# The branch for overfull experts stands at the end of its layer, and TensorE gets products that nobody reads

## The chip, the cores and the metric

One core of a Trainium2 chip runs the whole kernel. The metric is the time of one execution on the device, in microseconds, as the median of several runs. The time before is 2018.78 us, the median of three runs (2011.02, 2018.78 and 2019.69). The profiled execution is a run of its own: 2027.7 us, with a span of 2025.7 us from its first instruction to its last.

## The reference, cut to what matters

256 tokens of width 1024 pass through two networks, one after the other, in float32. The first has two layers. Each is an attention (the first a dilated one over three patterns, the second a "stick-breaking" one), a norm, a mixture of 16 experts with two chosen for each token, and a norm again:

```
x = layer_norm(ALPHA * x + attention(x))
x = layer_norm(ALPHA * x + sum over the two chosen experts e of
               weight[e] * (silu(x @ gate[e]) * (x @ up[e])) @ down[e])
```

The second network has two layers, each with a gated feed-forward part, a mixing part (a recurrence over the tokens, retention, latent attention and a short convolution side by side) and a second feed-forward part.

How many tokens an expert gets depends on the data. Nothing in the reference limits it.

## The kernel before, in words

**Products.** Most matrices are split into a high and a low part of a reduced float32 format (`split`, lines 238 to 241: ScalarE writes the high part, VectorE the difference), and a product is three products on TensorE (`mm3`, lines 243 to 247). A single product is `mm`, lines 249 and 250. Weights come by SyncE's queue into a ring of four raw tiles (`fetch`, line 221), are split into rings of five `whi` and five `wlo` tiles, and are used. Because the rings are short, a weight's load waits until the tile's last reader is done.

**Order.** The program is written as one stream, and a framework orders it: for each engine it picks, instruction by instruction, what is ready by its own model of time, with the earlier line first, and sets the semaphores. `keep_in_program_order` and `issue_after` tie an instruction to its place, `manual_schedule` does so for all of VectorE's in a block. A tile that reuses the memory of another waits for the other's last reader. PSUM tiles come from three rings: `psA` (four banks in most stages), `psB` and `psC` (two each). Rows of 1024 come from two rings of four: `x` for the state between stages, taken in pairs, one for each half of the tokens (`new_x`), and `row` for everything else.

**The expert layer** (`moe`, from line 814). The weights of all experts, 96 loads of 512 KB, go through one ring of 22 homes: the raw tiles, the `whi` and `wlo` tiles (named `wf` here) and eight tiles of the layer's own. The router's scores come from `product` in `attention_out` (line 465). VectorE then ranks the experts (lines 859 to 878), TensorE counts each token's rank within its expert (line 891 reads it), and VectorE builds `P`, a matrix with a one where a token sits in one of 64 places of an expert. `gather` multiplies the split tokens (`xsh`, `xsl`) with `P` and so collects each expert's tokens: 32 products of 512 columns for the first eight experts, four for each block of 128 features; the first eight products (`t0`) stand ahead of the branch, the other 24 behind it. Then eight rounds, two experts in each: `up` (line 941), the gating (`hidden`), the second matrix, and `back`, which puts the results back on their tokens with `P` transposed; `add` (line 960) adds them to the state `x`, scaled by ALPHA the first time. The last two rounds are added at line 999, and `layer_norm` (from line 411) makes the next state `y`; its statistics (line 418) are written into the head of `y`. The norm of the second half of the tokens is left to the next stage (`rest`).

**The branch** (lines 921 to 923). An expert with more than 64 tokens does not fit into its places. The largest count is read into a register of each engine, and if it is over 64, `overflow` (line 1018) computes what was left out for all 16 experts, with weights that SyncE loads again into `row` tiles. With these inputs nobody takes the branch. Where it is skipped, each engine jumps over its part of the body and then raises its semaphores by what the body would have raised them. What comes later in the program and uses a tile that the body uses waits for these.

**Other stages that the change touches.** `dilated` (line 568) is the kernel's first stage. `stick` (line 678) is the second attention: ten steps, in which projections, scores (`weights`) and values of different head pairs overlap. `mixers` (line 1105) computes its column blocks with `chunk`; after the third and the fourth, `p8` collects the squared length of the keys by small products with `hsel`.

Of the kernel before, what the change touches and what calls it, by code (L numbers as in the profile page):

```python
# [169 lines left out]
class Net:  # L170
# [80 lines left out]

    def proj_b(self, out, w, c0, n, x, ks=range(8)):

        for k in ks:
            s = slice(c0 + k * n, c0 + (k + 1) * n)
            self.mm3(out, (w[0][:, s], w[1][:, s]), (x[0][:, k, :], x[1][:, k, :]), k == 0, k == 7)
# [181 lines left out]
    def attention_out(self, x, yT, w, l):  # L438
# [24 lines left out]
        def product(c):  # L463
            for k in range(8):
                self.mm(p[:, :16], xf[c][:, k * 128:(k + 1) * 128], self.gr[:, k, :], k == 0, k == 7)
# [102 lines left out]
    def dilated(self, c1):  # L568
        nc, A = self.nc, self.A
        with self.tc.tile_pool(name="dil", bufs=1) as sp, self.tc.tile_pool(name="dr", bufs=1, space=bass.MemoryType.DRAM) as dr:  # L570
            self.sp = sp
            nc.scalar.preload_act_table_set("exp_and_others")
            xT = self.new_T()
            xf = [self.row() for _ in range(2)]
# [103 lines left out]
    def stick(self, x):  # L678
        nc, A = self.nc, self.A
        with self.tc.tile_pool(name="sb", bufs=1) as sp:  # L680
# [79 lines left out]
            with self.psum(512) as self.pa:  # L760
                qk, z = {}, {}
                for hp in range(10):
# [6 lines left out]
                    if 1 <= hp <= 8:  # L769
                        z[hp - 1] = weights(*qk.pop(hp - 1))  # L770
                    if hp >= 2:
# [42 lines left out]
    def moe(self, x, l):  # L814
# [4 lines left out]
        with self.tc.tile_pool(name="moe", bufs=1) as sp, self.psum(512) as self.pa:  # L819
# [21 lines left out]

# [12 lines left out]
            h0, h1 = self.halves  # L854

# [64 lines left out]

            rv = nc.values_load(ci[0:1, 0:1], min_val=0, max_val=256)
            with self.tc.If(rv > 64):
                self.overflow(x, l, rank, gt)

# [35 lines left out]
            def add(ns):  # L960
                for c in range(2):
                    acc = [self.psA() for _ in range(2)]
                    back(acc, c, ns, True, True)
                    for s, a in zip(self.halves, acc):
                        stt(out=x[c][:, s], in0=x[c][:, s], scalar=1.0 if ns[0] else ALPHA, in1=a, op0=OP.mult, op1=OP.add)

            p = up(0)
            for n in range(8):
# [26 lines left out]
            y, gb = self.new_x(), self.ln_rows(l, 1)  # L995
            for c in range(2):
                with self.tc.issue_after(self.end.ins) if c else ExitStack():
                    for s, a in zip(self.halves, acc[c]):
                        tt(out=x[c][:, s], in0=x[c][:, s], in1=a, op=OP.add)
                if c == 0:  # L1000
                    self.layer_norm(x[0], gb, y[0], True)
        self.rest = lambda: self.layer_norm(x[1], gb, y[1])
# [15 lines left out]
    def overflow(self, x, l, rank, gt):  # L1018
# [4 lines left out]
        XT = sp.tile([128, 8, 1024], F32, name="XTo", tag="XT")[:, :, :256]  # L1023
        for c in range(2):
            for k in range(0, 8, 4):
# [3 lines left out]
                self.evac(XT[:, k:k + 4, c * 128:c * 128 + 128], t.rearrange("p (j s) -> p j s", j=4))  # L1029
        y = self.acc()  # L1030

        def load(ap):
            for j in range(2):
                raw = self.row()
                nc.sync.dma_start(out=raw, in_=ap[:, j * 1024:j * 1024 + 1024])
                yield raw

        for e in range(16):
            p = [self.psC() for _ in range(2)]
            for b in range(2):  # L1040
                for j, w in enumerate(load(self.A["egu"][l, e, b])):
# [702 lines left out]
```

## Time and profile before

| | before |
|---|---|
| median of three runs | 2018.78 us |
| profiled execution, time | 2027.7 us |
| its span | 2025.7 us |
| mean granted clock of TensorE | 0.968 |
| TensorE busy | 1919.8 us, 95% |
| VectorE busy | 1186.3 us, 59% |
| ScalarE busy | 862.8 us, 43% |
| read from HBM | 353.53 MB, 175 GB/s |

The page of the profile lists busy time by engine, then the span in 40 slices, then queues, a chain of waits and the costliest groups. PE is TensorE's products, PEld its loads of the stationary operand, DVE VectorE, ACT ScalarE, POOL GpSimd, SP SyncE; a q behind the name is that engine's sequencer. In a row, `out<-in` names the tiles; in square brackets stands the idle time of the engine ahead of the instruction and what ended it. PEclk is the share of 2.4 GHz that TensorE was granted.

### The profile page before, as it was taken

The page shows a single profiled execution, that of the slowest core. Times are in us where ns is not written, and L with a number is a line of the kernel's source. Part 1 is how long each engine was busy: PE and PEld are TensorE (multiplying, and loading weights), DVE is VectorE, ACT ScalarE, POOL GpSimd, SP SyncE. Part 2 cuts the span into 40 slices and gives each one's busy share as a digit, 9 for nine tenths or more (in the row PEclk, how much of TensorE's full clock was granted, in tenths as well). Part 3 has the DMA queues.
Part 4 walks back from the last instruction along what each step waited for, and adds up shares of the span by engine and source line. Part 5 has one row for each costly group of instructions (what it writes and reads, how often), then busy time and mean ns, then how long its engine had stood idle before and what let it go on. Part 6 is the DMA issues. An engine that isn't in the chain of part 4 may idle for free. (4 is left out here: it accounts for less than half of the span.)

```text
span 2025.7 us, 36997 instructions
## 1 busy us (share of the span) xinstructions
PE 1919.8 (95%) x14866; PEld 1622.0 (80%) x14866; DVE 1186.3 (59%) x2329; ACT 862.8 (43%) x1786; POOL 193.3 (10%) x225
## 2 busy tenths in 40 slices
PE   7999997997897997999999999999999999999998
PEld 7999996434885443899888988998999888888997
DVE  6778775125876124855576556555555675556554
ACT  5656552112662112544543335445544533235443
POOL 1323220000220000000021100000000030100000
PEclk9999998998998998999998999999999999899999
DMA  8345346795436796655532215555555532215553
GB/s 280 126 137 164 127 135 240 278 408 191 146 125 222 268 388 232 211 188 187 184 113 77 93 62 178 185 188 168 199 187 188 188 103 83 84 61 176 189 186 107
DMA packets 102516, 357.10 MB, mean 176 GB/s; under 512 B 11888, under 2 KB 15136, under 8 KB 102208
## 3 DMA queue, kind: packets, MB, share of 16 engines
q1 hardware_dynamic: 97584, 341.70, 49.1%
q10 hardware_dynamic: 4704, 12.81, 2.0%
q8 instruction: 120, 1.97, 0.4%
q14 instruction: 60, 0.49, 0.1%
q0 software_dynamic: 48, 0.13, 0.0%
HBM read 353.53 MB, written 1.07 MB: 175 GB/s over the span
## 5 line engine op out<-in xcount | busy, mean ns | idle before, releaser
L241 DVE TENSOR_TENSOR wlo<-raw,whi 128x512 fp32r<-128x512 f32 (+1 forms) x910 | 626.1, 715 | 384.0 <-ACT whi L240 380.1
L240 ACT ACTIVATE whi<-raw 128x512 fp32r<-128x512 f32 (+1 forms) x910 | 529.8, 616 | 592.3 <-issue 197.6
L245 PE MATMUL psB<-xTh,whi 128*128 128x256 f32 x1792 | 507.7, 283 | 12.3 <-ACT whi L240 8.3
L247 PE MATMUL psB<-xTh,wlo 128*128 128x256 f32 x1792 | 506.4, 283 | 0.2 <-DVE wlo L241 0.2
L246 PE MATMUL psB<-xTl,whi 128*128 128x256 f32 x1792 | 506.1, 282 | 0.4
L245 PEld LDWEIGHTS psB<-xTh,whi 128*128 128x128 f32 x1792 | 340.1, 190 | 18.1 <-ACT whi L240 9.8
L246 PEld LDWEIGHTS psB<-xTl,whi 128*128 128x128 f32 x1792 | 340.1, 190 | 5.4 <-DVE xTl L241 1.5
L247 PEld LDWEIGHTS psB<-xTh,wlo 128*128 128x128 f32 x1792 | 340.3, 190 | 1.4 <-DVE wlo L241 0.7
L247 PE MATMUL psA<-whi,hl 128*128 128x512 f32 x352 | 139.5, 396 | 0.0
L245 PE MATMUL psA<-whi,hh 128*128 128x512 f32 x352 | 139.4, 398 | 0.0
L246 PE MATMUL psA<-wlo,hh 128*128 128x512 f32 x352 | 138.7, 394 | 0.0
L245 PE MATMUL psA<-xTh,whi 128*128 128x256 f32 (+1 forms) x352 | 107.8, 307 | 0.3 <-ACT vt L536 0.2
L247 PE MATMUL psA<-xTh,wlo 128*128 128x256 f32 (+1 forms) x352 | 105.1, 299 | 0.0
L246 PE MATMUL psA<-xTl,whi 128*128 128x256 f32 (+1 forms) x352 | 103.6, 295 | 0.3 <-DVE xTl L241 0.3
L245 PE MATMUL psB<-whi,xTh 128*128 128x384 f32 (+2 forms) x256 | 90.3, 353 | 3.6 <-DVE qs L547 1.7
L247 PE MATMUL psB<-whi,xTl 128*128 128x384 f32 (+2 forms) x256 | 88.7, 347 | 0.4 <-DVE xTl L241 0.3
L246 PE MATMUL psB<-wlo,xTh 128*128 128x384 f32 (+2 forms) x256 | 88.5, 346 | 0.3 <-DVE wlo L241 0.3
L296 POOL TENSOR_TENSOR ss<-ss,mh 128x1 f32<-128x1 f32 x14 | 9.8, 702 | 785.5 <-DVE ss L295 780.8
L250 PE MATMUL psB<-raw,XT 128*64 128x512 f32 x288 | 83.5, 601 | 0.0
L247 PEld LDWEIGHTS psA<-whi,hl 128*128 128x128 f32 x352 | 66.0, 188 | 16.8 <-DVE hl L241 0.7
L246 PEld LDWEIGHTS psA<-wlo,hh 128*128 128x128 f32 x352 | 66.6, 189 | 12.6
L245 PEld LDWEIGHTS psA<-whi,hh 128*128 128x128 f32 x352 | 66.3, 188 | 12.8 <-ACT hh L240 0.9
(414 smaller groups left out, 3036.1 us busy)
## 6 DMA issues: line engine op xcount, KB each, us to landing
raw<-in_ffn1gu_dram SPq DMA_DIRECT2D x88, 512.0 KB, 3.8
raw<-in_ffn2gu_dram SPq DMA_DIRECT2D x88, 512.0 KB, 3.7
raw<-in_egu_dram SPq DMA_DIRECT2D x72, 512.0 KB, 9.9
wf<-in_egu_dram SPq DMA_DIRECT2D x56, 512.0 KB, 8.6
raw<-in_dqk_dram SPq DMA_DIRECT2D x46, 512.0 KB, 3.9
raw<-in_ffn1dn_dram SPq DMA_DIRECT2D x44, 512.0 KB, 3.6
raw<-in_ffn2dn_dram SPq DMA_DIRECT2D x44, 512.0 KB, 3.6
raw<-in_wb_dram SPq DMA_DIRECT2D x40, 512.0 KB, 3.7
```

The costliest lines, as they stand in the source:

```text
L240: self.hi = self.nc.scalar.activation(hi, src, AF.Copy)
L241: return (self.nc.gpsimd if pool else self.nc.vector).tensor_tensor(out=lo, in0=src, in1=hi.bitcast(F32), op=OP.subtract)
L245: mm(out, a[0], b[0], start=start, stop=False)
L246: mm(out, a[0], b[1], start=False, stop=False)
L247: mm(out, a[1], b[0], start=False, stop=stop)
L250: return self.nc.tensor.matmul(out, a, b, start=start, stop=stop)
L296: nc.gpsimd.tensor_tensor(out=ss[:, 3:4], in0=ss[:, 2:3], in1=self.mh[:, :1], op=OP.pow)
```

## The change

The branch moves from behind the first gathers to behind the last `back`. Its register is read after the first `up`. The layer's sum now grows in a pair of `x` tiles of its own, `z`, so that `x` stays as the branch needs it. The body of the branch handles the halves of the tokens one after the other, loads each expert's weights once for each half, takes the raw tiles for them in place of `row` tiles, and adds into `z`. A function `busy` issues products into a `psC` tile that nobody reads; it is called in `dilated` (four in float32 at the kernel's start), in `stick` (eight, once), in each expert layer (nine, tied behind the router's last product) and in each `mixers` (eight, behind its fourth column block).

```diff
--- before.py
+++ after.py
@@ -249,6 +249,13 @@
     def mm(self, out, a, b, start=True, stop=True):
         return self.nc.tensor.matmul(out, a, b, start=start, stop=stop)
 
+    def busy(self, n, a, b, behind=None):
+
+        with self.tc.issue_after(behind.ins) if behind is not None else ExitStack():
+            t = self.psC()
+            for _ in range(n):
+                self.mm(t[:, :b.shape[-1]], a, b)
+
     def proj_b(self, out, w, c0, n, x, ks=range(8)):
 
         for k in ks:
@@ -462,7 +469,7 @@
 
         def product(c):
             for k in range(8):
-                self.mm(p[:, :16], xf[c][:, k * 128:(k + 1) * 128], self.gr[:, k, :], k == 0, k == 7)
+                self.scored = self.mm(p[:, :16], xf[c][:, k * 128:(k + 1) * 128], self.gr[:, k, :], k == 0, k == 7)
             nc.vector.scalar_tensor_tensor(out=lg[:, c, :], in0=p[:, :16], scalar=mv[c][:, 2:3], in1=self.br, op0=OP.mult, op1=OP.add)
 
         acc = self.out_proj(yT, w, rows)
@@ -571,6 +578,9 @@
             self.sp = sp
             nc.scalar.preload_act_table_set("exp_and_others")
             xT = self.new_T()
+            w = self.row()[:, :512]
+            nc.gpsimd.memset(w, 1.0)
+            self.busy(4, w[:, :128], w)
             xf = [self.row() for _ in range(2)]
             for i in range(4):
                 nc.scalar.dma_start(out=xf[i // 2].rearrange("p (k t) -> p k t", k=4)[:, i % 2 * 2:i % 2 * 2 + 2, :],
@@ -768,6 +778,8 @@
                         self.tc.keep_in_program_order(nc.scalar.preload_act_table_set("natural_log_exp_and_others"))
                     if 1 <= hp <= 8:
                         z[hp - 1] = weights(*qk.pop(hp - 1))
+                    if hp == 2:
+                        self.busy(8, xT[0][:, 0, :128], xT[0][:, :2, :].rearrange("p k t -> p (k t)"))
                     if hp >= 2:
                         values(hp - 2, z.pop(hp - 2))
                 return self.attention_out(x, yT, A["so"], 1)
@@ -838,7 +850,6 @@
                 for e, i, ap in ts:
                     raws[e, i] += self.fetch(ap, ring=ring)
 
-
             fetch(todo[:len(homes)])
             sc = sp.tile([128, 32], F32, name="sc")
             bi = sp.tile([128, 32], F32, name="bi")
@@ -852,6 +863,7 @@
             b4 = bi.rearrange("p (g e) -> p g e", e=4)
             scale, shift = self.steps
             h0, h1 = self.halves
+            self.busy(9, self.ones_r, xs[0][0][:, h0], self.scored)
 
             with self.tc.manual_schedule(engines={mybir.EngineType.DVE}):
 
@@ -917,11 +929,6 @@
                 return t
 
             t0 = [gather(k, 0, self.psB()) for k in range(2)]
-
-            rv = nc.values_load(ci[0:1, 0:1], min_val=0, max_val=256)
-            with self.tc.If(rv > 64):
-                self.overflow(x, l, rank, gt)
-
             fetch(todo[len(homes):])
             XT = sp.tile([128, 8, 1024], F32, name="XT")
             for k in range(8):
@@ -962,9 +969,14 @@
                     acc = [self.psA() for _ in range(2)]
                     back(acc, c, ns, True, True)
                     for s, a in zip(self.halves, acc):
-                        stt(out=x[c][:, s], in0=x[c][:, s], scalar=1.0 if ns[0] else ALPHA, in1=a, op0=OP.mult, op1=OP.add)
-
+                        if ns[0]:
+                            tt(out=z[c][:, s], in0=z[c][:, s], in1=a, op=OP.add)
+                        else:
+                            stt(out=z[c][:, s], in0=x[c][:, s], scalar=ALPHA, in1=a, op0=OP.mult, op1=OP.add)
+
+            z = self.new_x()
             p = up(0)
+            rv = nc.values_load(ci[0:1, 0:1], min_val=0, max_val=256)
             for n in range(8):
                 h = self.hidden(p, gw[:, n:n + 1])
                 if n < 7:
@@ -992,14 +1004,18 @@
             for i in range(2):
                 for c in range(2):
                     back(acc[c], c, (7,), False, True, (i,))
-            y, gb = self.new_x(), self.ln_rows(l, 1)
+            gb = self.ln_rows(l, 1)
+
+            with self.tc.If(rv > 64):
+                self.overflow(x, z, l, rank, gt)
+            y = self.new_x()
             for c in range(2):
                 with self.tc.issue_after(self.end.ins) if c else ExitStack():
                     for s, a in zip(self.halves, acc[c]):
-                        tt(out=x[c][:, s], in0=x[c][:, s], in1=a, op=OP.add)
+                        tt(out=z[c][:, s], in0=z[c][:, s], in1=a, op=OP.add)
                 if c == 0:
-                    self.layer_norm(x[0], gb, y[0], True)
-        self.rest = lambda: self.layer_norm(x[1], gb, y[1])
+                    self.layer_norm(z[0], gb, y[0], True)
+        self.rest = lambda: self.layer_norm(z[1], gb, y[1])
         return y
 
     def places(self, out, rank):
@@ -1015,43 +1031,40 @@
             self.split(xs[0][0][:, s], xs[0][1][:, s], x[0][:, s])
         return xs
 
-    def overflow(self, x, l, rank, gt):
+    def overflow(self, x, z, l, rank, gt):
 
         nc, v, sp = self.nc, self.nc.vector, self.sp
         g2 = sp.tile([128, 2, 16], F32, name="gt2")
         v.scalar_tensor_tensor(out=g2, in0=rank, scalar=64.5, in1=gt, op0=OP.is_gt, op1=OP.mult)
-        XT = sp.tile([128, 8, 1024], F32, name="XTo", tag="XT")[:, :, :256]
+        XT = sp.tile([128, 8, 1024], F32, name="XTo", tag="XT")
+        y = [self.psA() for _ in range(2)]
+
+        def load(ap):
+            for j in range(2):
+                raw = self.wp.tile([128, 1024], F32, name="raw", bufs=self.nraw)
+                nc.sync.dma_start(out=raw, in_=ap[:, j * 1024:j * 1024 + 1024])
+                yield raw
+
         for c in range(2):
+            xT = XT[:, :, c * 128:c * 128 + 128]
             for k in range(0, 8, 4):
                 t = self.psC()
                 for j in range(4):
                     nc.tensor.transpose(t[:, j * 128:j * 128 + 128], x[c][:, (k + j) * 128:(k + j) * 128 + 128], self.ident)
-                self.evac(XT[:, k:k + 4, c * 128:c * 128 + 128], t.rearrange("p (j s) -> p j s", j=4))
-        y = self.acc()
-
-        def load(ap):
-            for j in range(2):
-                raw = self.row()
-                nc.sync.dma_start(out=raw, in_=ap[:, j * 1024:j * 1024 + 1024])
-                yield raw
-
-        for e in range(16):
-            p = [self.psC() for _ in range(2)]
-            for b in range(2):
-                for j, w in enumerate(load(self.A["egu"][l, e, b])):
+                self.evac(xT[:, k:k + 4, :], t.rearrange("p (j s) -> p j s", j=4))
+            for e in range(16):
+                p = self.psC()
+                for b in range(2):
+                    for j, w in enumerate(load(self.A["egu"][l, e, b])):
+                        for i in range(2):
+                            k = 4 * b + 2 * j + i
+                            self.mm(p, xT[:, k, :], w[:, i * 512:i * 512 + 512], k == 0, k == 7)
+                hT = self.hidden_T(self.hidden(p, g2[:, c, e:e + 1]))
+                for j, w in enumerate(load(self.A["edn"][l, e])):
                     for i in range(2):
-                        k = 4 * b + 2 * j + i
-                        for c in range(2):
-                            self.mm(p[c], XT[:, k, c * 128:c * 128 + 128], w[:, i * 512:i * 512 + 512], k == 0, k == 7)
-            hs = [self.hidden(p[c], g2[:, c, e:e + 1]) for c in range(2)]
-            hs = [self.hidden_T(h) for h in hs]
-            for j, w in enumerate(load(self.A["edn"][l, e])):
-                for c in range(2):
-                    for i in range(2):
-                        self.mm(y[c][i], hs[c][:, j, :], w[:, self.halves[i]], e == 0 and j == 0, e == 15 and j == 1)
-        for c in range(2):
-            for s, a in zip(self.halves, y[c]):
-                v.scalar_tensor_tensor(out=x[c][:, s], in0=a, scalar=1.0 / ALPHA, in1=x[c][:, s], op0=OP.mult, op1=OP.add)
+                        self.mm(y[i], hT[:, j, :], w[:, self.halves[i]], e == 0 and j == 0, e == 15 and j == 1)
+            for s, a in zip(self.halves, y):
+                v.tensor_tensor(out=z[c][:, s], in0=z[c][:, s], in1=a, op=OP.add)
 
 
     def second_consts(self, pool):
@@ -1223,6 +1236,8 @@
             p8 = self.psC()
             for h in range(2):
                 p = chunk(2 + h)
+                if h:
+                    self.busy(8, xT[0][:, 0, :128], xT[0][:, :2, :].rearrange("p k t -> p (k t)"))
                 self.evac(kT[h], p[:, :256])
                 ts(kk[h], kT[h], par(4, h), None, op0=OP.mult)
                 sq = new("t")
```

## Rows read from the trace of the kernel before

**Rows 1.** The page: busy time, share and instructions; clock by slices, in tenths.

```profile
PE 1919.8 (95%) x14866; PEld 1622.0 (80%) x14866; DVE 1186.3 (59%) x2329; ACT 862.8 (43%) x1786; POOL 193.3 (10%) x225
...
PEclk9999998998998998999998999999999999899999
```

**Rows 2.** The branch's line: count, duration in ns (min/median/max), first and last start.

```profile
L922 SPq COMPARE_BRANCH  x2: 50/52/53, 338.4 to 647.6; - x2
...
L922 PEldq COMPARE_BRANCH  x2: 6052/6070/6088, 340.7 to 650.5; - x2
```

**Rows 3.** Timeline around the first branch, TensorE: start, duration (us), what.

```profile
340.09 1.05 PE L250 MATMUL psB<-P,xsl 128*128 128x512 f32 x2
...
348.38 0.63 PE L250 MATMUL psA<-P,xsl 128*128 128x512 f32 x1
348.81 0.63 PE L250 MATMUL psA<-P,xsh 128*128 128x512 f32 x1
```

**Rows 4.** Timeline: the last gathers and the first expert products.

```profile
353.94 0.39 PE L250 MATMUL psA<-P,xsl 128*128 128x512 f32 x1
354.17 0.39 PE L250 MATMUL psA<-P,xsh 128*128 128x512 f32 x1
...
354.73 1.94 PE L250 MATMUL psB<-raw,XT 128*64 128x512 f32 x8
```

**Rows 5.** Waits for weights in the loop, 355 to 485: us, times, longest.

```profile
PEld psB L250 <- DMA wf<-in_egu_dram: 1.8, 5, 0.4
```

**Rows 6.** Windows: length, busy PE PEld DVE ACT POOL, clock, DMA share, GB/s.

```profile
331.55:335.45 3.90, 0.00 (x0) 0.00 (x0) 3.17 (x19) 0.23 (x1) 0.00 (x0) 0.50 1.03 417
650.60:664.85 14.25, 8.12 (x25) 6.20 (x24) 4.02 (x7) 3.02 (x5) 0.00 (x0) 0.60 0.61 229
532.30:535.15 2.85, 0.00 (x1) 0.00 (x0) 2.73 (x5) 0.84 (x2) 0.00 (x0) 1.00 0.01 4
535.65:539.05 3.40, 3.33 (x17) 2.96 (x16) 3.31 (x7) 3.32 (x6) 1.49 (x3) 0.50 0.00 0
1036.90:1039.60 2.70, 0.00 (x0) 0.00 (x1) 2.70 (x9) 0.00 (x0) 1.78 (x2) 1.00 0.03 12
1040.84:1047.66 6.82, 6.82 (x33) 5.33 (x33) 1.97 (x4) 0.47 (x1) 0.00 (x0) 0.50 0.71 223
15.10:20.25 5.15, 4.98 (x21) 4.69 (x22) 5.02 (x9) 4.89 (x10) 0.00 (x0) 1.00 0.64 208
20.25:25.30 5.05, 5.05 (x45) 5.05 (x44) 4.33 (x8) 3.38 (x8) 1.57 (x2) 1.00 0.87 267
```

**Rows 7.** Timeline at the end of the first expert layer.

```profile
484.25 0.39 PE L250 MATMUL psB<-yel,PT 128*128 128x512 f32 x1
...
485.20 1.28 DVE L418 BATCH_NORM_STATS2 x<-x 128x6 f32<-128x512 f32 x2
...
486.40 0.67 DVE L241 TENSOR_TENSOR wlo<-raw,whi 128x512 fp32r<-128x512 f32 x1
486.99 0.20 DVE L420 BATCH_NORM_AGGREGATE ss<-x 128x2 f32<-128x12 f32 x1
...
489.94 0.87 PE L266 MATMUL psC<-c0t,x 128*128 128x128 f32 x3 [5.30 <-DVE x L427]
```

**Rows 8.** Timeline at the end of the second expert layer.

```profile
795.86 1.28 DVE L418 BATCH_NORM_STATS2 x<-x 128x6 f32<-128x512 f32 x2
```

**Rows 9.** The raw tile, 455 to 500: its loads (ns, first to last start), landing.

```profile
L221 SPq DMA_DIRECT2D raw<-in_sv_dram x4: 327/328/328, 473.0 to 475.5; - x4
...
DMA to landing us min/median/max: 4.0/5.6/6.6
```

**Rows 10.** Timeline of the start: TensorE's first product, ScalarE's wait for weights.

```profile
7.69 0.58 PE L245 MATMUL psB<-xTh,whi 128*128 128x256 f32 x1 [7.69 <-ACT whi L240]
...
50.18 1.15 ACT L240 ACTIVATE whi<-raw 128x512 fp32r<-128x512 f32 x2 [3.70 <-DMA raw<-in_dqk_dram]
```

**Rows 11.** Timeline of the first mixers: VectorE behind the small products.

```profile
1027.07 0.17 DVE L1233 TENSOR_SCALAR ss<-psC 128x8 f32<-128x8 f32 x1 [0.43 <-PE psC L250]
```

## The prediction

> **What bounds the kernel now.** I read the page first. TensorE is busy for 95% of the span, and its clock line stands at 9 or 8 tenths in most slices [rows 1]: time is to be had where TensorE stands idle, or works at the lower of its two clock levels (0.5 of 2.4 GHz, that is 1.2). Next came the line of the branch. Nobody takes it, yet TensorE's sequencer spends 6.05 to 6.09 us on it in each of the two expert layers, and SyncE's 0.05 us [rows 2]. Then the order of time around it: the last pair of gathers before the branch ends at 340.09 + 1.05 = 341.14 us, and those after it run 0.43 us apart at first [rows 3] and 0.23 us apart at the end; the first expert product starts at 354.73 us [rows 4]. Behind that the loop over experts is TensorE's: the largest group of its waits on weights is 1.8 us in all [rows 5], so what is won ahead of the loop arrives at its end. The windows give the rest [rows 6]: with columns of busy time, clock, DMA share and GB/s they show the second layer's stall and its 24 gathers (together 14.25 us, of which TensorE is busy for 8.12, at clock 0.60), and seven idle or half-rate stretches that I come to below. Last, the layer's end: TensorE's last product starts at 484.25, VectorE's statistics at 485.20, and TensorE's next work, the transposes of the following stage, at 489.94 us [rows 7].
>
> **The change part by part.** The sums are against the profiled execution, 2027.7 us (span 2025.7). It lies 8.9 us above the median of the three runs, 2018.78, so I carry the difference over to the median.
>
> *The branch leaves the middle.* In the first layer 24 gathers can follow the first eight at once: 341.14 + 24 x 0.235 (the spacing at the full clock) = 346.8 us, where the first expert product now starts at 354.73: 7.9 us. In the second, 650.6 + 5.6 = 656.2 against 664.85, the ends of that window [rows 6]: 8.6 us. Together **16.5 us**. The bounds: with all 24 at the low spacing of 0.43 the gathers take 10.3 us and the gain falls to 3.3 and 3.9; above, no more than the stall and half of the gathers' low-clock time, 9 each. I take the upper part because the gathers then follow each other without a stall, and because the nine products placed ahead of the ranking hold 9 x 0.43 = 3.9 us, just the 3.90 us in which TensorE is idle there at clock 0.50 [rows 6]; they are in nobody's way at the low clock and half as long at the high one. The register load moves along and stays beside other work; its four companions on the other engines wait for nothing that is late.
>
> *The branch arrives at the end.* TensorE reaches it when its last product of the layer is out (484.25) and leaves it near 484.3 + 6.1 = 490.4. Until then TensorE would stand idle anyway, for 5.30 us [rows 7]. But the cover is not free. The sum of the layer now needs a pair of row buffers of its own (z), so all four are taken, and the pair for the result (y) is the one that holds x, which the branch's body reads on TensorE. VectorE's first statistic writes into y; it starts at 485.20 now and has to wait for 490.4: **5.2 us late**, with the transposes of the next stage behind it. The second layer's end has the same order (statistics at 795.86 [rows 8], last product 0.95 us earlier if it keeps the first layer's distance), so 5.2 again: +10.4 us. Below, the delay could be 1 us (if the two halves of the weight split that stand within that chain drop out of it); above, 8, if the next stage's weights come too late as well. The body now takes its weights through the ring of raw weights that the next stage's prefetch uses, so SyncE can issue that prefetch only behind the branch; today it does from 473.0 on [rows 9]. The cover for this is the norm itself, which takes from 485.20 to 489.94 = 4.7 us.
>
> A page speaks against moving the branch at all. The Trainium skill, "Runtime: NRT & Kernel Launch", section "Instruction fetch mechanics", says that a taken branch whose target lies outside what is loaded makes the engine fetch the target's page before it goes on, wherever the branch stands. The trace agrees for TensorE, with its 6.05 to 6.09 us, and not for the other engines. By that rule alone the whole stall is paid again at the end, 12.1 us for 10.4, and the result would be 1.7 us later than mine.
>
> So the branch is worth -16.5 + 10.4 = **-6.1 us**. The additions of the layer keep their count and form (z in place of x): nothing.
>
> *The start.* Four float32 products of 512 columns on a tile that GpSimd fills. Eight half-products side by side in pairs take 1.94 us [rows 4], 0.485 a pair; these fill the whole width, so 8 x 0.485 = 3.9 us, 7.8 at the low level. TensorE's first real product starts at 7.69 us [rows 10] with nothing before it, so they fit to within a microsecond. The gain is later: from 15.10 to 20.25 us 21 products run, from 20.25 on 45 in as long [rows 6] (the clock column shows 1.00 for both; the doubled pace says that the first stretch was at the low level). At most half of 5.15 = 2.6 us; but ScalarE waits 3.70 us for a weight to land at 50.18 [rows 10], where much of it is lost. I take **-1**; bounds -2.6 and +0.8.
>
> *The second attention.* Eight products of 0.23 = 1.9 us in a gap of 2.85 us before the transposes of the first values; behind it stands a stretch of 3.40 us at clock 0.50 with TensorE full [rows 6], of which 1.7 can be won. VectorE is busy for 3.31 us of it, so I take **-1**; bounds -1.7 and +1.9 (if the products land elsewhere).
>
> *The mixers, twice.* Eight products, 1.9 us, behind the fourth column block, where TensorE is not idle. VectorE waits for the small products after it, at 1027.07 for 0.43 us [rows 11], and could be made late by 1.9 - 0.4 = 1.5. On the other side, TensorE idles 2.70 us at 1036.90, and then works 6.82 us at clock 0.50 [rows 6]; work shifted into that gap may keep the clock up and win 3.4. Between +1.5 and -3.4 per layer I take the middle, -1: **-2**.
>
> Sum: -6.1 - 1 - 1 - 2 = **-10.1**: 2017.6 against 2027.7, and 2018.8 - 10.1 = **2008.7 us** against the median, 0.5% faster.
>
> **The rivals.** *The clock holds everywhere* (faster). Start -2.6, attention -1.7, mixers -6.8, branch as above: -17.2, 2001.6 us. For it: each of these stretches is TensorE's own work at half rate. Against: only the products of the expert layers are tied to a place; the others have none, and VectorE is near full around two of them.
>
> *The norm waits for weights* (slower). In VectorE's queue two halves of a weight split (486.40 the first) stand between the statistics and their aggregate at 486.99 [rows 7]. If that order stays, the aggregate waits for weights that are issued only behind the branch. The raw loads of this stretch have a median of 5.6 us from issue to landing [rows 9]: 490.4 + 0.6 + 5.6, and then ScalarE's and VectorE's halves of the split, 0.6 + 0.7, give 497.9 for 487.0. That is 10.9 us a layer in place of 5.2. The sum is then -10.1 + 11.4 = +1.3: 2020 us, and with the mixers' and the attention's bounds on the bad side 2028. It decides from the point where the aggregate stands behind a split of the next stage. For it: the queue of today; against: the order is made anew, and a split whose weights come later moves back.
>
> *The products do not do what they are for.* They lie where TensorE was working, or leave the clock as it is; the gathers stay at the low spacing in part (gain 11 for 16.5), and nothing comes from the other three places: -11 + 10.4 = -0.6, 2018 us.
>
> **How the numbers follow.** The forecast 0.42, with 2003 to 2015 as its own range (gathers at the low clock for a third of their time, or the norm's chain a microsecond shorter); the clock everywhere 0.28; the norm behind weights 0.14; products without effect 0.16. A measurement of this kernel can tell about 0.5%, 10 us, from no change. Faster by more: all of the second and half of the first, 0.48; slower by more: most of the norm's case, 0.11; the rest, 0.41. Eight in ten lie between 1996, just past the clock's case, and 2025, in the norm's.
>
> **What would show it.** Right: the branch still takes 6 us on TensorE but lies behind the layer's last product; the first expert product starts 8 us sooner after the ranking; the statistics start when the branch ends, 5 us later after that product than now. The clock's case: no stretch at 0.50 near 0.51 and 0.81 of the span. The norm's case: an idle stretch of VectorE before the aggregate, ended by ScalarE's half of a split. Wrong from the ground up: statistics that do not wait for TensorE's branch (then 10 us more are won), or a first expert product that is no sooner.

## The result, and the profile after

The changed kernel is slower by 0.9%, where 0.5% faster was forecast.

| | before | after |
|---|---|---|
| median of six runs | 2016.37 us | 2037.51 us (2028.97 to 2041.63) |
| ratio | | 1.0092, 95% interval 1.0068 to 1.0115 |
| profiled execution, its span | 2027.7, 2025.7 us | 2041.63, 2039.8 us |
| mean granted clock, profiled execution | 0.968 | 0.963 |

The profiled execution of before lies 11 us above its median, that of after 4, so the traces show only 14 of the 21 us. One execution of the runs below, of e9 (2053.5 us), counts as slow and is left out of its ratio. The page of the changed kernel, as [rows 1]: TensorE is busy 26.6 us longer. The 50 added products (those 4 in float32 count double) account for some 19 of that: 6.19 at the start, 4.19 and 3.30 in the expert layers, 1.9 in each of three other places. The rest fits the old work at a lower clock.

```profile
PE 1946.4 (95%) x14916; PEld 1642.9 (81%) x14916; DVE 1190.7 (58%) x2329; ACT 862.4 (42%) x1786; POOL 196.6 (10%) x226
...
PEclk9999998998999997999989999999999988999999
```

To see where, I matched the instructions of VectorE and ScalarE that both traces have, in order, and took how much later each starts after than before. The change of that over a stretch (times of before) is what the stretch cost:

| stretch of before, us | what | forecast | in the trace |
|---|---|---|---|
| 0 to 310 | start and first attention | -1 | +0.1 |
| 310 to 352 | ranking and gathers, first layer | -7.9 | -6.4 |
| 352 to 478 | its loop over experts | 0 | +3.3 |
| 478 to 525 | its end, start of the next stage | +5.2 | +9.9 |
| 525 to 630 | second attention | -1 | +0.3 |
| 630 to 670 | ranking and gathers, second layer | -8.6 | -10.8 |
| 670 to 785 | its loop | 0 | +1.3 |
| 785 to 830 | its end | +5.2 | +7.8 |
| 990 to 1150 | first mixers | -1 | +7.3 |
| 1590 to 1870 | second mixers | -1 | -0.4 |
| the rest | | 0 | +1.6 |

**The middle.** The timeline of TensorE after: the first expert products of the two layers and the small products behind the first (start, duration, what). They start 7.95 us sooner than [rows 4], and 3.5 us sooner than [rows 6] although everything was 7.3 late by then.

```profile
346.78 1.94 PE L250 MATMUL psB<-raw,XT 128*64 128x512 f32 x8
348.64 4.78 PE L250 MATMUL psC<-gt,P 128*128 128x16 f32 x32
...
661.34 1.94 PE L250 MATMUL psB<-raw,XT 128*64 128x512 f32 x8
```

**The end of the first layer.** The branch's line after, to be held against [rows 2], then who waited for it:

```profile
L1009 PEldq COMPARE_BRANCH  x2: 3387/3546/3705, 481.4 to 793.0; - x2
...
  PE psA L250: 8.0, 2
```

TensorE's timeline there. In brackets stands its idle time and what ended it; compare [rows 7].

```profile
480.90 0.39 PE L250 MATMUL psB<-yel,PT 128*128 128x512 f32 x1
485.38 0.77 PE L250 MATMUL psA<-yel,PT 128*128 128x512 f32 x1 [4.09 <-PEq L1009]
485.95 0.63 PE L250 MATMUL psB<-yel,PT 128*128 128x512 f32 x1
490.63 1.94 PE L273 MATMUL psC<-c0t,x 128*128 128x128 f32 x8 [4.05 <-DVE x L434]
495.64 0.55 PE L245 MATMUL psB<-whi,xTh 128*128 128x256 f32 x1 [3.07 <-issue]
497.31 0.58 PE L245 MATMUL psB<-whi,xTh 128*128 128x256 f32 x1 [1.11 <-ACT whi L240]
```

The branch is shorter than before, but two products of the layer stand **behind** it. Then comes the norm (4.05 us), and then a wait of 3.07 us that the late weights cause. The other queues in the same stretch (SyncE, VectorE, ScalarE):

```profile
485.36 3.12 SPq L221 DMA_DIRECT2D raw<-in_sv_dram  x4
...
486.79 1.28 DVE L425 BATCH_NORM_STATS2 x<-x 128x6 f32<-128x512 f32 x2
...
489.28 1.15 ACT L240 ACTIVATE whi<-raw 128x512 fp32r<-128x512 f32 x2 [9.25 <-DMA raw<-in_sv_dram]
493.91 1.15 ACT L240 ACTIVATE whi<-raw 128x512 fp32r<-128x512 f32 x2 [3.49 <-DMA raw<-in_sv_dram]
494.97 0.58 ACT L240 ACTIVATE xTh<-psC 128x512 fp32r<-128x512 f32 x1
```

SyncE passes its own branch at 458.5 us, but the four loads for the next stage leave at 485.36, just behind TensorE's branch, where they left from 473.0 [rows 9]: the raw tiles count as read by the body of the branch, on TensorE. ScalarE idles 9.25 us for them, and 3.49 us again for the next. The product at 495.64 does not wait for its own weights, whose split is out at 490.4: it waits for the high part of the tokens (`xTh`), which stands behind two more splits of late weights in ScalarE's queue and is out at 495.55. The second layer repeats it: 3.88 us at the branch, then 7.46 us until the transposes at 805.16.

The clock takes part as well. Around both ends TensorE works at half clock for longer, first after, then before:

```profile
484.20:501.30 17.10, 7.67 (x28) 6.10 (x29) 10.90 (x19) 5.45 (x10) 0.99 (x1) 0.50 0.58 188
794.90:818.70 23.80, 11.10 (x28) 7.86 (x29) 18.94 (x35) 9.27 (x20) 4.08 (x5) 0.50 0.63 224
```

```profile
487.88:494.70 6.82, 4.76 (x21) 4.54 (x22) 6.47 (x11) 2.74 (x5) 0.99 (x1) 0.50 0.34 108
798.50:808.70 10.20, 4.68 (x14) 3.45 (x15) 10.13 (x19) 5.70 (x12) 2.46 (x3) 0.50 0.42 157
```

This is no accident of one execution. From 465 to 530 us and from 770 to 840 all seven traces with the branch in its old place have 13.7 and 10.2 us at half clock, and the four that keep the changed kernel's end as it is (the change, e1, e15, e16) have 20.5 to 23.9 us in either.

**The products.** Windows after (columns as in [rows 6]): the start, the stretch behind the first expert product, and the first and second mixers.

```profile
6.37:13.20 6.83, 4.88 (x21) 2.78 (x19) 3.28 (x5) 2.93 (x5) 0.00 (x0) 1.00 1.03 379
13.20:20.03 6.83, 5.36 (x23) 5.07 (x24) 5.32 (x10) 5.03 (x10) 0.00 (x0) 0.50 0.81 301
20.03:25.05 5.02, 5.02 (x44) 5.02 (x43) 3.59 (x6) 3.49 (x8) 1.57 (x2) 1.00 0.54 149
...
351.12:357.95 6.83, 6.83 (x24) 4.05 (x23) 0.33 (x2) 0.60 (x1) 0.00 (x0) 0.50 0.31 111
...
1042.57:1045.24 2.67, 2.67 (x24) 2.27 (x21) 2.67 (x8) 1.42 (x3) 1.54 (x2) 1.00 0.69 256
1047.44:1064.50 17.06, 17.06 (x132) 14.44 (x132) 7.69 (x15) 1.41 (x3) 2.27 (x2) 0.50 0.29 93
1661.84:1672.08 10.24, 10.24 (x105) 8.97 (x104) 5.27 (x10) 0.00 (x0) 2.27 (x2) 0.50 0.32 103
```

At the start the clock is up for 6.83 us behind the four products, falls again for 6.83, and is up for good at 20.03 us, where it was before too (20.25). In the first mixers the half clock lasts 17.06 us where it lasted 6.82 [rows 6]: products of a narrow column block (weights of 32 columns) that ran in that stretch now run ahead of TensorE's idle stretch (the 2.67 us row), and what is left behind it is a chain of small ones.

### The profile page after: what moved, and what is told of

Read it like the earlier page. It is cut to its first block, busy times and chain, and to the rows that moved or that the text cites. A ratio compares the mean times of both kernels' runs of the same rounds, so it can differ in the third digit from the quotient of the medians.

```text
span 2039.8 us, 37085 instructions
## 1 busy us (share of the span) xinstructions
PE 1946.4 (95%) x14916; PEld 1642.9 (81%) x14916; DVE 1190.7 (58%) x2329; ACT 862.4 (42%) x1786; POOL 196.6 (10%) x226
## 5 line engine op out<-in xcount | busy, mean ns | idle before, releaser
L245 PE MATMUL psB<-whi,xTh 128*128 128x384 f32 (+2 forms) x256 | 91.7, 358 | 10.4 <-issue 5.4
L245 PEld LDWEIGHTS psA<-whi,hh 128*128 128x128 f32 x352 | 66.4, 189 | 12.4 <-ACT hh L240 0.9
## 6 DMA issues: line engine op xcount, KB each, us to landing
raw<-in_egu_dram SPq DMA_DIRECT2D x72, 512.0 KB, 10.2
```

The costliest lines, as they stand in the source:

```text
L245: mm(out, a[0], b[0], start=start, stop=False)
```

## The experiments

All ratios are against the kernel before on the same chip, with 95% intervals. The clock is the median over the runs of the mean granted clock; that of before was 0.972 to 0.975. Kernels with the start's products show 0.0017 too little beside the others, since the records of the others have no clock ahead of some 20 us (6.83 us at half rate are listed in the one and not in the other).

| run | branch | products | ratio | clock |
|---|---|---|---|---|
| the change | end | all | 1.0092 (1.0068 to 1.0115) | 0.967 |
| e1 | end | none | 1.0054 (1.0033 to 1.0074) | 0.971 |
| e2 | old place | all | 1.0077 (1.0046 to 1.0108) | 0.967 |
| e3 | end, own tiles | all | 1.0026 (1.0005 to 1.0047) | 0.971 |
| e4 | end, tied | all | 1.0088 (1.0059 to 1.0116) | 0.966 |
| e5 | end, free | all | 1.0054 (1.0030 to 1.0078) | 0.970 |
| e6 | end, free | none | 0.9975 (0.9955 to 0.9996) | 0.977 |
| e7 | end, free | nine | 1.0004 (0.9987 to 1.0020) | 0.976 |
| e8 | old place | mixers | 1.0058 (1.0035 to 1.0080) | 0.970 |
| e9 | old place | none, order of e8 | 1.0032 (1.0000 to 1.0065) | 0.970 |
| e10 | old place | mixers, order of before | 1.0032 (1.0005 to 1.0060) | 0.974 |
| e11 | old place | nine | 1.0023 (1.0000 to 1.0045) | 0.974 |
| e12 | old place | start, attention | 1.0040 (1.0021 to 1.0059) | 0.971 |
| e13 | end, own tiles | none | 1.0011 (0.9988 to 1.0034) | 0.975 |
| e14 | end, free norm | none | 1.0017 (0.9995 to 1.0039) | 0.975 |
| e15 | end | all but mixers | 1.0044 (1.0020 to 1.0068) | 0.968 |
| e16 | end | all but start, attention | 1.0068 (1.0047 to 1.0090) | 0.968 |

**e1 and e2, each half alone.** e1 takes out the four calls of `busy`; e2 puts them into the kernel before.

> The branch at the end of its layer, without any of the added products. Theory A (the end of the layer takes back what the middle wins): in the changed kernel the middle won 8 to 11 us a layer, and the end lost 9 and 8 (two last products behind the branch, weights of the next stage asked for only after it). Without the nine products ahead of the ranking the gathers run longer at the low clock, so the middle wins 4 to 8: 5 to 15 us over the kernel before. Rival B (the added products cost the 21 us, the branch's move is the gain that was forecast): 6 us under the kernel before.

> The kernel before, branch in its old place, with all five groups of added products. Theory A: the mixers of the first layer lose 7 us (the order after their products is another and the clock stays low for 17 us in place of 7), the second attention 1, the start nothing, the second mixers nothing; the nine products of the expert layers win 0 to 2 each: 4 to 9 us over the kernel before. Rival B: 20 us and more over it.

e1: 10.9 us over before; e2: 15.5. Theory A holds for e1, and rival B is out, since the move is no gain. But the products cost 15 us, not the 4 to 9 that I read from one profile. Both halves lose, and by more than the change does: 0.54% and 0.77% against 0.92% for both together, so the two losses do not simply add.

**e3 and e4, two ties of the layer's end.** e3, in the body's loads:

```diff
-                raw = self.wp.tile([128, 1024], F32, name="raw", bufs=self.nraw)
+                raw = sp.tile([128, 1024], F32, name="raw2", bufs=RAW2)
```

e4, where `last` is the product that `back` issued last:

```diff
-            rv = nc.values_load(ci[0:1, 0:1], min_val=0, max_val=256)
...
+            with self.tc.issue_after(self.last.ins):
+                rv = nc.values_load(ci[0:1, 0:1], min_val=0, max_val=256)
             with self.tc.If(rv > 64):
```

> The changed kernel, but the body of the branch takes its weights into the expert layer's own eight tiles in place of the raw tiles that the next stage's loads use. Theory A: the loads for the second attention leave SyncE near 470 us again, 15 us sooner, TensorE's waits of 3.1 and 1.1 us ahead of its first products go, likewise in the second layer: 8 us under the changed kernel. Rival C (the two late products and the wait of the statistics set the end, the weights are late beside them): within 2 us of it.

> The changed kernel, but the branch's register is read behind the layer's last product, so the branch is TensorE's next instruction after it. Theory A: the two products come 4 us sooner, but the statistics go into tiles that the branch's body reads, so they start when TensorE's branch is out (near 485.3 for 486.8), and the next stage's weights are as late as before: 0 to 3 us under the changed kernel. Rival C: 8 us under it.

e3 is 13 us under the change, more than expected; e4 is where the change is. e4's trace shows the forecast's own mechanism, the statistics that wait for TensorE's branch, and then the late weights (VectorE, then TensorE; for the 3.53 us see the wait for `xTh` above):

```profile
484.74 1.29 DVE L425 BATCH_NORM_STATS2 x<-x 128x6 f32<-128x512 f32 x2 [2.82 <-PEq L1010]
...
488.59 1.94 PE L273 MATMUL psC<-c0t,x 128*128 128x128 f32 x8 [8.13 <-DVE x L434]
494.06 0.55 PE L245 MATMUL psB<-whi,xTh 128*128 128x256 f32 x1 [3.53 <-issue]
```

**e5 to e7, the end free.** Both edits, and a norm that the body cannot hold up: `y` is `z`, written in place, and the first half's statistics get a tile of their own (the second half's go into the old `x`).

```diff
-            y = self.new_x()
+            y = z
+            st = sp.tile([128, 12], F32, name="st"), x[1][:, :12]
```

e5 has all products, e6 none, e7 the nine of each expert layer.

> The changed kernel with all three ties of the layer's end taken off: the body's weights in the layer's own tiles, the branch behind TensorE's last product, and the norm written over the sum itself with its statistics in a tile of their own, so that nothing of it waits for the branch's body. Theory A (the 4 to 6 us that the branch costs TensorE are then hidden beside the norm): TensorE's next work starts near 485.5 in place of 490.6, and the weights are there: 9 us a layer under the changed kernel, near 2020 us. Rival C (the end has another limit behind these three, as the next stage's loads or the norm of the second half): no better than the kernel with the body's own tiles, 2026 us.

> The same without any of the added products. Theory A (the products cost about 10 us, mostly by a lower mean clock): 8 to 14 us under the kernel with a free end and all products, 2006 to 2012 us, and 7 to 13 under the kernel before the change; mean clock 0.973 or more. Rival D (the products only move work, and their loss of clock is the chance of one execution): the same as with all products, within 4 us.

> The same with the nine products of the expert layers alone. By the forecast they keep the gathers at the high clock, worth 3 to 4 us a layer: 6 to 8 under the kernel with a free end and no products. Rival E (they shift TensorE's work at half clock to the stretch behind, as in the run with the branch in its old place, where each layer lost 2.5 us): 0 to 5 us over it.

e6's end of the first layer (VectorE, TensorE): the last product starts at 481.59 us, the branch begins at 482.1 and takes 3.46 us, and neither the norm nor the weights wait for it. TensorE's idle time is 5.04 us, about as it was with no branch there (5.30, [rows 7]).

```profile
483.19 1.28 DVE L425 BATCH_NORM_STATS2 st<-x 128x6 f32<-128x512 f32 x2
...
487.03 1.94 PE L273 MATMUL psC<-c0t,x 128*128 128x128 f32 x8 [5.04 <-DVE x L434]
488.85 0.77 PE L245 MATMUL psB<-whi,xTh 128*128 128x256 f32 x2
```

The second end is not as free. TensorE, before, then TensorE and VectorE in e6:

```profile
803.99 1.94 PE L266 MATMUL psC<-c0t,row 128*128 128x128 f32 x8 [8.69 <-DVE row L298]
```

```profile
805.30 1.94 PE L273 MATMUL psC<-c0t,row 128*128 128x128 f32 x8 [12.49 <-DMA c2t<-in_c_dram]
804.40 1.42 DVE L305 SCALAR_TENSOR_TENSOR row<-x,ss,row 128x512 f32<-128x512 f32 x2 [0.44 <-POOL ss L303]
```

The profile names the load of `c2t`, but in each of e5, e6 and e7 the transposes start 0.9 us behind the start of VectorE's `row`, as before the change. It is `row` that is late: VectorE now takes the second half's statistics and two splits of weights ahead of its scale.

e6 beats both kernels: 0.25% under the one before, 5 us where 7 to 13 were expected. e5 is 16 us over e6, by the products alone. It is also no better than e3 (1.0054 against 1.0026, on another chip), as rival C had it: with the products in, the free norm brought nothing that shows. e7 is 6 over e6, on rival E's side, though the two intervals just overlap.

**e13 and e14, the two ties singly, without products.** With e1 and e6 they make a square: e13 is e1 with e3's edit, e14 is e6 without it. Its corners ran on three chips, each against the kernel before on its own.

> The move of the branch without any added product, with the body's weights in the expert layer's own tiles. Theory W (the weights behind the branch are most of the end's loss): 7 to 11 us under the move alone (which was 11 over the kernel before), so 0 to 4 over the kernel before. Theory N (late products and late statistics are as much): 3 to 5 under the move alone, 6 to 8 over the kernel before.

> The move without any added product, with the branch tied behind TensorE's last product and the norm free of the branch's body, but the body's weights again through the raw tiles of the next stage. Theory W: no better than the move alone, 8 to 11 us over the kernel before. Theory N: 4 to 7 over it.

| | norm waits | norm free |
|---|---|---|
| weights wait | 1.0054 | 1.0017 |
| weights free | 1.0011 | 0.9975 |

Either tie costs about 0.4%, 8 us over both layers, give or take 0.3%: both edits are needed. e13 came out where theory W had it, e14 below both theories. Whether the two costs simply add, these intervals can't tell. TensorE in e13, then in e14: in the one the branch holds up the last products and the norm, and the weights are there; in the other the norm is in time, and the weights (by way of `xTh` again) are 5.29 us late.

```profile
481.39 0.47 PE L250 MATMUL psA<-yel,PT 128*128 128x512 f32 x1 [3.93 <-PEq L1003]
481.70 0.55 PE L250 MATMUL psB<-yel,PT 128*128 128x512 f32 x1
486.35 1.94 PE L273 MATMUL psC<-c0t,x 128*128 128x128 f32 x8 [4.09 <-DVE x L434]
```

```profile
488.45 1.90 PE L273 MATMUL psC<-c0t,x 128*128 128x128 f32 x8 [5.06 <-DVE x L434]
495.63 0.55 PE L245 MATMUL psB<-whi,xTh 128*128 128x256 f32 x1 [5.29 <-issue]
```

**e8 to e12, the products by groups in the kernel before.** e8, e11 and e12 keep some calls of `busy`. e9 has none; it writes the narrow block earlier (`p21 = chunk(21)` behind `chunk(6)`). e10 is e8 with that block tied behind the products that TensorE idles for.

> The kernel before with the eight products in each mixers stage and nothing else. Theory A (of the products' loss the mixers bear the most, 6 us in the first, 0 to -5 in the second, by the order that follows and the clock): 3 to 7 us over the kernel before, mean clock 0.002 lower. Rival D: within 2 us of it.

> The kernel before with no added product; in each mixers stage the 24 products of 32 columns (weight tile 128x32) are written earlier, so that they run ahead of TensorE's idle stretch and not behind it, the order that the mixers' products brought about. Theory F (the mixers lose by that order: behind the idle stretch stand only small products that wait for each other, and the clock stays at half for 14 to 17 us in place of 7): 4 to 8 us over the kernel before, low stretch 10 us or longer in both mixers. Rival G (they lose by their own time and what they shift): within 2 us of it.

> The kernel before with the mixers' products, and those 24 products tied behind TensorE's idle stretch, where the kernel before has them. Theory F: 1.9 us for the eight products in each stage and nothing else, 2 to 5 us over the kernel before (the products alone gave 11.7). Rival G: 9 us and more over it.

> The kernel before, branch in its old place, with the nine products of the expert layers alone. Theory H (they raise the clock ahead of the gathers, but the branch's 6 us of idle TensorE takes it down again, so they bring nothing): within 3 us of the kernel before. Rival I (they cost by themselves, as the run with a free end and the nine, 5 us over the one without, would have it): 4 to 6 us over it.

> The kernel before with the products of the kernel's start and of the second attention alone. From the profiles so far: the attention's cost 1 to 2.5 us, the start's 0 to 1 (the clock is up for 7 us after them and falls again before it rises for good at the same 20 us): 1 to 3 us over the kernel before. What the forecast had: 2 us under it.

No group gains: mixers 0.58%, start and attention 0.40%, the nine 0.23%, the last with an interval that reaches down to no cost. The first two are more than I had read from profiles (12 us for 3 to 7, 8 for 1 to 3), and the three together are more than all products at once cost in e2 (0.77%). The stretch at half clock in the first mixers, in e8, e9 and e10:

```profile
1043.89:1057.54 13.65, 13.65 (x117) 11.29 (x115) 5.92 (x11) 1.41 (x3) 2.27 (x2) 0.50 0.28 84
```

```profile
1047.36:1057.60 10.24, 10.24 (x106) 9.10 (x105) 6.05 (x11) 1.15 (x2) 3.34 (x4) 0.50 0.27 96
```

```profile
1045.03:1051.86 6.83, 6.83 (x33) 5.68 (x33) 1.92 (x4) 0.00 (x0) 0.00 (x0) 0.50 0.51 149
```

With the old order restored the stretch is short again, and with the order alone it is long: theory F's mechanism is there. But both runs stand at 0.32%, about half of e8's cost each, and their intervals, from next to nothing to all of it, are too wide to part order and own time. e9's runs spread from 2013 to 2042 us.

In e11 the nine bring the clock up, but only for 3.43 us; then it is down until 350.58, through the branch and most of the 24 gathers behind it (TensorE works 7.75 of 13.65 us):

```profile
333.50:336.93 3.43, 1.85 (x9) 1.23 (x9) 3.19 (x11) 0.63 (x1) 0.00 (x0) 1.00 1.03 412
336.93:350.58 13.65, 7.75 (x18) 5.57 (x19) 5.27 (x8) 2.17 (x4) 0.00 (x0) 0.50 0.73 267
```

That the clock is lost is theory H's outcome, but not by its cause: the clock falls 1.6 us before the branch begins (338.5 us), while TensorE works on and off. The time, 4.6 us over the kernel before, is nearer to rival I, and the interval holds both.

**e15 and e16, groups taken out of the change.**

> The changed kernel without the mixers' products. If they cost in it what they cost in the kernel before (11.7 us): 0.3 to 0.4% over the kernel before in place of 0.9%. If the clock's chances around them are others there: 0.6 to 0.8%.

> The changed kernel without the products of the start and of the second attention. If they cost in it what they cost in the kernel before (8 us): 0.5 to 0.6% over the kernel before. By their profiles alone (2 to 4 us): 0.7 to 0.8%.

The mixers' products cost 0.48% in the changed kernel, the start's and attention's 0.24%, somewhat less than alone but within the intervals; e16 is nearer to what the profiles had for its groups than to e12's time. Over the 18 profiled executions the stretch of the first mixers (1030 to 1095 us) is 4.7 us longer with its products (7 traces) than without (9; e9 and e10 left out), with 15.6 us at half clock for 6.8; the second (1590 to 1670) 3.2 longer; the attention 2.1 and the start 1.3.

## Why the prediction was wrong

**The branch leaves the middle: half right.** The first expert product came at 346.78 us, the 346.8 of the sum, and at 661.34 with 7.3 us of delay carried, 10.8 won for 8.6. What was won is the stall; the nine products, the sum's second reason for the upper part, have little share in it. From the router's last product to the first expert product it takes 22.6 and 24.3 us in the five traces with the branch in its old place and no nine, 15.4 and 15.7 in the four with the branch moved and no nine, 14.6 and 14.3 in the seven with the branch moved and the nine. The failed step is "what is won ahead of the loop arrives at its end". In the first layer 5.0 of the 7.95 us went in the loop. Its product at 480.90 comes 2.9 us sooner than before, where it is this one:

```profile
483.80 0.39 PE L250 MATMUL psB<-yel,PT 128*128 128x512 f32 x1
```

The clock falls for 6.83 us behind the small products (about 3 us), and TensorE waits about 1 us for VectorE three times in place of two. (VectorE and ScalarE, by which the table goes, were 6.4 us sooner ahead of the loop, so it has 3.3.) Over all traces, 11 with the branch moved against 7 without, the two layers win 5.6 and 6.8 us up to the loop's end: **12.4 for 16.5**.

**The branch arrives at the end: the mechanism was right, and its neighbours were left out.** "TensorE reaches it when its last product of the layer is out" failed: two products stand behind it. And the weights, which I named and put into the bound of 8, are a cost of their own. The four traces with all ties (the change, e1, e15, e16) lose 7.0 and 8.3 us at the two ends, measured against the mean of the seven with the branch in its old place: **15.3 for 10.4**, of which the longer half clock is a part. The branch itself was cheaper than taken, 3.4 to 3.7 us for 6.1. The second rival had the late weights, but put them into the norm's chain; there the splits dropped out (statistics to transposes 3.84 us, for 4.74 before), and the wait came one step later, at the next stage's first products. With 12.4 and 15.3 in place of 16.5 and 10.4 the branch's -6.1 becomes +2.9 by the traces; by the runs it is +10.9 (e1).

**The added products: wrong in sign.** -4 was taken, and +0.4% (e1 against the change) to +0.8% (e2) was measured. "I take the middle" between +1.5 and -3.4 in the mixers failed: the products were costed at their own time, and not at what their 1.9 us does to the order behind them and to the clock. The start's -1 failed as well: the clock that they raised did not hold, and it was up for good no sooner than before. The third rival was nearest in kind, but gave the products no price.

**The range.** All bad bounds together (-7.2 + 16 + 0.8 + 1.9 + 3.0) give +14.5, 2033 us; the range was cut at 2025. What is missing even there no run prices by itself; the half clock at the ends and in the mixers, which no bound has, is the likely part.

**What stays open.** Each tie costs 8 us by the runs. By the ends of the traces, both layers together, freeing the weights alone wins 4.5 us of the 15.3 (e3, e13), freeing the norm alone 1.4 (e14), and both 12.4 (e5, e6, e7): there the two waits lie side by side, and either keeps the end late. The runs are too coarse to say which picture holds. Nor do the traces place all of the loss: 2.9 us of the branch's 10.9 stand in the four stretches, and where the rest stands is open; it may go with the mean clock (0.971 in e1, 0.977 in e6), at places that change with the execution. Whether the nine gain anything once the branch is out of the way is open too. e7 says 6 us lost; the change against e1, e15 and e16 (0.38% for all, 0.48 and 0.24 for the other two) leaves them a gain, and so do the traces with the branch moved: up to the loops' ends the seven with the nine are 5 us ahead of the four without, both layers together.

## What to carry to other kernels

A branch that nobody takes still owns the tiles that its body touches: before it is moved, list for each engine what stands behind it in the queue and which rings its body uses, and give the body rings whose next user is far away. Idle time at the new place hides a stall only if the work that ends this idle time does not pass through the branch. Look too at what stands between the late piece and its user: here weights held up the tokens, since one engine splits both in order. Products put in to keep a clock up showed no gain at any place that can be told from none, not even the nine, which are tied into an idle stretch; beside real work they take its time and change its order.

## What the runs showed of the hardware

**The same work at either clock, whatever the edit.** One stretch of the first mixers, which no edit touches, in the kernel before and in e6: the same 148 products take 13.65 us and 7.70.

```profile
1102.28:1115.93 13.65, 13.65 (x148) 12.96 (x148) 5.53 (x13) 3.14 (x9) 0.00 (x0) 0.50 0.23 80
```

```profile
1102.90:1110.60 7.70, 7.70 (x148) 7.28 (x148) 5.23 (x12) 2.79 (x9) 0.00 (x0) 1.00 0.20 71
```

Of the 18 executions 7 have these products at half clock, 13.65 us long; the other 11 have them at the full one, some with a half-clock stretch shortly before or behind. TensorE is busy through both stretches, and which execution has which does not follow the edits: the kernel before and e15 have it, e8 and e16 have not. Such stretches can be what spreads the runs of one kernel (2006 to 2032 us for the one before, over four chips), though no run shows it, and one profile tells nothing of 6 us. The Trainium skill, "TensorE: Matmul & The Clock Gate", section "Part 1: The HAM clock gate", says that how many products run at the low rate at a kernel's start changes from run to run; these rows show the like in mid-kernel, and say nothing of the start.

**The price of the untaken branch goes with the DMA traffic.** TensorE took 6.05 to 6.09 us for it at its old place [rows 2], 3.39 to 3.71 after, and between 3.33 and 6.19 in the other runs with the branch at the end. Windows of 3.3 us from the branch's start: the first branch before (6.09 us long), the second after (3.39), the second in e7 (6.19). The last two columns are the DMA share and GB/s.

```profile
340.70:344.00 3.30, 0.45 (x2) 0.00 (x0) 2.39 (x4) 0.63 (x1) 0.00 (x0) 0.94 1.02 410
```

```profile
793.00:796.30 3.30, 0.00 (x0) 0.00 (x0) 0.69 (x1) 0.00 (x0) 0.00 (x0) 0.78 0.03 7
```

```profile
783.50:786.80 3.30, 0.00 (x0) 0.00 (x0) 3.30 (x7) 0.44 (x1) 0.00 (x0) 1.00 0.59 205
```

The 36 branches of the 18 traces fall into place by that share: up to 0.16 they take 3.33 to 3.97 us (one 4.43), from 0.52 to 0.84 they take 4.15 to 6.19, from 0.96 on 5.53 to 6.37. So the branch was short at the layer's end where little was being loaded, and an edit that brings the next weights forward may make it longer again (5.07 us in e13's second layer, at a share of 0.55). No run changes the traffic alone, so this is a finding of rows, and the cause is not shown. The page on instruction fetch that the prediction weighed (the Trainium skill, "Runtime: NRT & Kernel Launch", "Instruction fetch mechanics") has the stall go with the branch, as a fetch by DMA; the stall was indeed met at every place, but not at one length, and no run shows the fetch.
